# Broadcast rows of the decode states stored by batch row and given four buffers, and the decode rows of x turned in the first stage

## The chip, the cores and the metric

One of the eight cores of a Trainium2 chip runs the whole program. The metric is device time in microseconds (us), of the one core. Lower is better. The kernel before has a median of 3007.94 us over three runs (3006.08 to 3008.26).

## The reference, cut to what matters

The reference is one inference step of a hybrid decoder layer in float32: gated DeltaNet and S5 branches side by side, merged by gates, then an FFN. It runs for a prompt of 512 tokens and for a decode group of 8 rows with one token each. The part that the change touches is the DeltaNet state of the decode group:

```python
def step(S, inp):                       # gated_delta_recurrent, one token
    q_t, k_t, v_t, b_t, g_t = inp
    S = S * jnp.exp(g_t)[..., None, None]
    v_new = (v_t - jnp.einsum('bhk,bhkv->bhv', k_t, S)) * b_t[..., None]
    S = S + jnp.einsum('bhk,bhv->bhkv', k_t, v_new)
    return S, jnp.einsum('bhk,bhkv->bhv', q_t, S)
```

and the residual `x = x + merged @ w_out`, for which the 8 decode rows of x are needed with features on the partitions.

## The kernel before, in words

All activations lie with features on the 128 partitions and 520 columns: 512 prompt tokens and the 8 decode rows. A product with a weight matrix (`product`, L80 to L96) computes 128 output features at a time. `weights` (L72 to L79) loads a tile `raw` of 128x8x128 numbers (512 KB), ScalarE splits off its high part `whi` (L78) and VectorE its low part `wlo` (L70), and TensorE runs three matmuls for each of 8 row blocks and each half of the columns: 48 matmuls of 128x260 for 8 row blocks. There are three `raw` buffers, two of `whi` and `wlo`, and two PSUM tiles `pt`, so that a product can start only when the result of the one two places earlier has been taken out of PSUM.

The program runs in stages: the input is normed and turned into `hhi`/`hlo` (L151 to L203); products with `w_in` run beside the S5 and DeltaNet branches; then products with `w_glu`, with `w_br_s5` (eight tiles in `s5_part`, result `m`, L1176), with `w_br_dn` (result `gd`, L1274), with `w_out`, and the FFN by a Strassen scheme (L1363).

The decode states are the generator `decode` (L729 to L807), whose steps are laid between the `w_glu` and `w_br_s5` products. The new values `vn` [128 (v), 64 (h b)] are turned on TensorE (`pvt`), copied to `vr` and written to DRAM as `vsc` [h, b, v]. Then for each of 8 batch rows b:

- SyncE issues `vb <- vsc[:, b]` (L802): 8 runs of 128 floats (512 bytes), 4 KB apart in DRAM, read once for every partition, 512 KB in all. `vb` has 2 buffers.
- GpSimd multiplies `vb` by the keys (L803), VectorE adds it to the state tile `st` (L805), SyncE stores `st` (L806, 512 KB).

`st` of all eight rows is loaded and scaled (L804) before. A like copy stands earlier in `prep` (L946): `dx <- xdsc` spreads 16 rows of 4 KB in DRAM over eight groups of 16 partitions, the eight copies being the outermost loop of its source, 512 KB too; its rows serve as a price below. Each `gs` (L1174) is a gate tile of 260 KB. All DMAs are issued by SyncE, in one queue. After the decode, L1251 to L1259 load the 8 decode rows of x again (`xd`), turn them by 16 small transposes on TensorE (`pdx`) and copy them to `xdt`; L1293 adds them to the residual.

The order of each engine's instructions is fixed when the program is built: a scheduler lays out the recorded instructions, and each engine then runs its list in order. A wait at the head of such a list therefore holds all that stands behind it.

Of the kernel before, what the change touches and what calls it, by code (L numbers as in the profile page):

```python
# [9 lines left out]
F32 = mybir.dt.float32  # L10
# [7 lines left out]
P = 128  # L18
D = 2048
NTOK = 512  # L20
NB = 8
T = NTOK + NB
HF = T // 2
KD = D // P
# [9 lines left out]
def hybrid_step_kernel(  # L34
# [9 lines left out]
    nc = tc.nc  # L44
    V, G, A, PE = nc.vector, nc.gpsimd, nc.scalar, nc.tensor
    xp = x_prompt[0]
    xs = x_sample.rearrange("b l d -> (b l) d")
# [6 lines left out]
    dp = ctx.enter_context(tc.tile_pool(name="dp", bufs=1, space=DRAM))  # L54
# [5 lines left out]
    def slot(name):  # L60
        return big.tile([P, 8, T], F32R, tag="slot", name=name)

    def pmt(name="m", tag="m"):
        return pm.tile([P, 512], F32, tag=tag, name=name)
# [34 lines left out]
    ident = cp.tile([P, P], F32, name="ident")  # L99
# [42 lines left out]
            V.tensor_copy(vecs[:, 1, 0:25], pv[:, P:P + 25])  # L142


    HT = []
    hhi = [slot("hhi0"), slot("hhi1")]
    hlo = [slot("hlo0"), slot("hlo1")]
    for k in range(KD):
        HT.append((hhi[k // 8][:, k % 8], hlo[k // 8][:, k % 8]))
    with tc.tile_pool(name="x0", bufs=1) as x0:  # L150
        xt = [x0.tile([P, D], F32, name=f"x{c}") for c in range(5)]  # L151
        ss = x0.tile([P, 5, 2], F32, name="ss")
        junk = x0.tile([P, D // 2], F32, name="junk")
        G.memset(ss, 1.0)
        A.activation(junk[0:1, 0:1], ss[0:1, 0, 0:1], AF.Square)
        for c in (4, 0, 1, 2, 3):
            n = P if c < 4 else NB
            src = xp[c * P:(c + 1) * P, :] if c < 4 else xs
            for cs in (slice(0, D // 2), slice(D // 2, D)) if c < 4 else (slice(0, D),):
                nc.sync.dma_start(xt[c][0:n, cs], src[:, cs])  # L160
            if c == 0:
                load_vectors()
        for c in (4, 0, 1, 2, 3):
            n = P if c < 4 else NB
            for j in range(2):
                A.activation(junk[0:n], xt[c][0:n, j * D // 2:(j + 1) * D // 2], AF.Square,
                             accum_out=ss[0:n, c, j:j + 1])
            rs = ss[:, c, 0:1]
            V.tensor_tensor(rs, rs, ss[:, c, 1:2], ALU.add)
            V.tensor_scalar(rs, rs, 1.0 / D, EPS, op0=ALU.mult, op1=ALU.add)  # L170
            rsqrt(rs)
            if c == 4:
                V.tensor_scalar(xt[4][0:NB], xt[4][0:NB], rs[0:NB], None, op0=ALU.mult)
                continue
            for j in range(4):
                cs = slice(j * D // 4, (j + 1) * D // 4)
                V.tensor_scalar(xt[c][:, cs], xt[c][:, cs], rs, None, op0=ALU.mult)

        def turn(c):
            for k0 in range(0, KD, 2):  # L180
                pk = pmt("pk", "me"[k0 // 2 % 2])
                for j in range(2):
                    for i in range(2):
                        PE.transpose(pk[:, (j * 2 + i) * P:(j * 2 + i + 1) * P],
                                     xt[c + i][:, (k0 + j) * P:(k0 + j + 1) * P], ident)
                for j in range(2):
                    k = k0 + j
                    hi, lo = (v[:, c * P:(c + 2) * P] for v in HT[k])
                    pj = pk[:, j * 2 * P:(j + 1) * 2 * P]
                    A.activation(hi, pj, AF.Copy, scale=n1[:, k:k + 1])  # L190
                    V.scalar_tensor_tensor(lo, pj, n1[:, k:k + 1], hi.bitcast(F32), op0=ALU.mult, op1=ALU.subtract)

        pdec = pmt("pdec")
        for k in range(KD):
            PE.transpose(pdec[:, k * NB:(k + 1) * NB], xt[4][0:NB, k * P:(k + 1) * P], ident[0:NB, 0:NB])
        hd = x0.tile([P, KD, NB], F32, name="hd")
        V.tensor_tensor(hd, pdec[:, 0:KD * NB].rearrange("p (k b) -> p k b", b=NB),
                        n1.unsqueeze(2).to_broadcast([P, KD, NB]), ALU.mult)
        for i in range(2):
            A.activation(hhi[i][:, :, NTOK:T], hd[:, i * 8:(i + 1) * 8], AF.Copy)  # L200
            lo_part(hlo[i][:, :, NTOK:T], hd[:, i * 8:(i + 1) * 8], hhi[i][:, :, NTOK:T])
        turn(0)
        turn(2)  # L203
# [16 lines left out]
    def beta_decay():  # L220
        with tc.tile_pool(name="bap", bufs=1) as bp:
# [3 lines left out]
            A.activation(bc[:, 0], bc[:, 0], AF.Exp)  # L225
            pt = product(w_in, 0, C_BA, HT)
            bsb = bp.tile([16, T], F32, name="bsb")
# [254 lines left out]
    def u_tile(i, upp):  # L482
        pt = product(w_in, 0, C_U + i * P, HT, by_half=i == 0)
        us = gp.tile([P, T], F32, tag="gtile", name="us")
# [11 lines left out]
    def gate_tile(t):  # L496
        j, i = t // KD, t % KD
        pt = product(w_in, 0, (C_GD, C_GS)[j] + i * P, HT)
        gt = gp.tile([P, T], F32, tag="gate", name="gate")
# [229 lines left out]
    def decode(dec, dd, de, ohi, olo):  # L729
# [37 lines left out]
        vn = t64("vn")  # L767
# [20 lines left out]
        A.activation(ohi[:, :, NTOK:T], odv, AF.Copy)  # L788
        lo_part(olo[:, :, NTOK:T], odv, ohi[:, :, NTOK:T])

        pvt = pmt("pvt")
        PE.transpose(pvt[0:64, 0:P], vn, ident)
        vr = dd.tile([64, P], F32, name="vr")
        V.tensor_copy(vr, pvt[0:64, 0:P])
        vsc = dp.tile([8, 8, P], F32, name="vsc")
        nc.sync.dma_start(vsc.rearrange("h b v -> (h b) v"), vr)
        knv = kn.rearrange("p (h b) -> p h b", h=8)
        egv = decv[:, 0]
        for b in range(NB):
            st = sts[b]  # L800
            vb = de.tile([P, 8, P], F32, name="vb")
            nc.sync.dma_start(vb, vsc[:, b].unsqueeze(0).to_broadcast([P, 8, P]))  # L802
            G.tensor_tensor(vb, vb, knv[:, :, b:b + 1].to_broadcast([P, 8, P]), ALU.mult)  # L803
            V.tensor_tensor(st, st, egv[:, :, b:b + 1].to_broadcast([P, 8, P]), ALU.mult)  # L804
            V.tensor_tensor(st, st, vb, ALU.add)  # L805
            nc.sync.dma_start(s_dn_ssm[0, b].rearrange("h k v -> k h v"), st)  # L806
            yield  # L807
# [384 lines left out]
    fin = fin_s.enter_context(tc.tile_pool(name="fin", bufs=1))  # L1192
# [56 lines left out]
            A.activation(hi, src, AF.Copy, scale=scale)  # L1249
            V.scalar_tensor_tensor(lo, src, scale, hi.bitcast(F32), op0=ALU.mult, op1=ALU.subtract)  # L1250

    with tc.tile_pool(name="xdp", bufs=1) as xdp:
        xdt = fin.tile([P, KD, NB], F32, name="xdt")
        xd = xdp.tile([NB, D], F32, name="xd")
        nc.sync.dma_start(xd, xs)
        pdx = pmt("pdx")
        for k in range(KD):
            PE.transpose(pdx[:, k * NB:(k + 1) * NB], xd[:, k * P:(k + 1) * P], ident[0:NB, 0:NB])
        V.tensor_copy(xdt.rearrange("p k b -> p (k b)"), pdx[:, 0:KD * NB])  # L1259
    with tc.tile_pool(name="mp", bufs=8) as mp, tc.tile_pool(name="mq", bufs=2) as mq:  # L1260
        add_squares, rstd = squares(mq)
        for m in range(2):
# [21 lines left out]
            for t in range(KD):  # L1284
                a = acc(t)
                if m == 0:
                    xt = mq.tile([P, 4, P], F32, name="xt")
# [20 lines left out]
                else:  # L1308

                    q = t - 8  # L1310
                    b = acc(q)
# [116 lines left out]
    for q in range(8):  # L1428
        b = acc(q)
# [132 lines left out]
    with ExitStack():  # L1562
# [152 lines left out]
        for c in range(4):  # L1715
            for h in range(2):
                v = yt[c][:, h * D // 2:(h + 1) * D // 2]
# [41 lines left out]
```

## Time and profile before

| what | value |
|---|---|
| median of three runs | 3007.94 us |
| profiled execution, its own time | 3003.06 us |
| its span (first to last instruction) | 3001.3 us |
| TensorE busy | 2884.6 us, 96% |
| VectorE, ScalarE, GpSimd busy | 68%, 43%, 38% |
| mean granted TensorE clock | 0.979 |

The page of the profile gives busy shares and the chain that ended last: work followed back from the last instruction, at each step to what released it. The trace can be asked for one stretch, one engine or one tile. In its rows a time is microseconds from the start of the span; in brackets stands how long the engine was idle before, and what ended that. "DMA share" is the mean busy share of the 16 DMA engines. The profiled execution took 3003.06 us, 4.9 us (0.16%) less than the median.

### The profile page before, as it was taken

How to read it: one execution, taken by the hardware profiler on the slowest of the kernel's cores; microseconds unless marked ns; L12 is line 12 of the kernel's file. 1: busy time of each engine (PE TensorE's matmuls, PEld its weight loads, DVE VectorE, ACT ScalarE, POOL GpSimd, SP SyncE). 2: the span in 40 equal slices, each digit the busy share in tenths (PEclk: the TensorE clock that was granted, in tenths of full speed). 3: DMA queues.
4: the chain of work that ended last, by engine and by line, in shares of the span. 5: the costliest groups of instructions: out<-in, count | busy, mean ns of one | idle time of the engine just before them, and what ended most of it. 6: DMA issues, size and time to landing. Idle time of an engine off the chain costs nothing.

```text
span 3001.3 us, 60983 instructions
## 1 busy us (share of the span) xinstructions
PE 2884.6 (96%) x23869; PEld 2848.7 (95%) x23869; DVE 2043.5 (68%) x3405; ACT 1279.8 (43%) x2229; POOL 1132.9 (38%) x1656
## 2 busy tenths in 40 slices
PE   7999999899999999699998999999999999999997
PEld 7999999899999999699998999999999998999997
DVE  5767444344554334243458899999999988999997
ACT  5244433233333222022244555555555555445555
POOL 0674403654444300210133454555555444222233
PEclk9999999999999998899999999999999999999999
DMA  6454444223333364754444455555555548765542
GB/s 163 107 126 127 120 129 102 73 70 75 81 77 82 96 181 115 181 150 117 135 128 127 138 163 166 166 167 161 161 168 162 160 151 284 260 206 168 185 139 86
DMA packets 647701, 424.17 MB, mean 141 GB/s; under 512 B 66525, under 2 KB 597694, under 8 KB 643774
## 3 DMA queue, kind: packets, MB, share of 16 engines
q1 hardware_dynamic: 647414, 420.28, 48.4%
q8 instruction: 188, 3.08, 0.4%
q14 instruction: 99, 0.81, 0.1%
HBM read 342.85 MB, written 75.12 MB: 139 GB/s over the span
## 4 chain that ended last, share of the span: by engine, by line
PE 76%; POOL 8%; DMA 6%; DVE 5%; issue 2%; ACT 1%; SPq 1%; POOLq 0%; ACTq 0%; DVEq 0%
PE pt L94 30%; PE px L1363 23%; PE py L1363 12%; PE pz L1363 6%; POOL tm L953 2%; DVE wlo L70 2%; POOL uu L955 2%; DMA vb<-vsc 2%; DMA dx<-xdsc 2%; PE pss L904 1%; POOL et L598 1%; DVE ac L1635 1%; POOL et L597 1%; PE psk L761 1%; DVE sm L1352 0%
## 5 line engine op out<-in xcount | busy, mean ns | idle before, releaser
L70 DVE TENSOR_TENSOR wlo<-raw,whi 128x512 fp32r<-128x512 f32 (+1 forms) x485 | 523.9, 1095 | 241.5 <-ACT whi L78 194.4
L78 ACT ACTIVATE whi<-raw 128x1024 fp32r<-128x1024 f32 x218 | 231.0, 1060 | 669.0 <-PE pt L94 597.3
L94 PE MATMUL pt<-hhi,wlo 128*128 128x260 f32 (+2 forms) x2336 | 492.6, 289 | 2.7 <-DVE wlo L70 2.5
L94 PE MATMUL pt<-hlo,whi 128*128 128x260 f32 (+2 forms) x2336 | 493.2, 289 | 0.0
L94 PE MATMUL pt<-hhi,whi 128*128 128x260 f32 (+1 forms) x2336 | 490.2, 289 | 1.4 <-ACT pre L866 1.3
L94 PEld LDWEIGHTS pt<-hhi,wlo 128*128 128x128 f32 x2336 | 369.3, 191 | 6.3 <-DVE wlo L70 4.1
L94 PEld LDWEIGHTS pt<-hhi,whi 128*128 128x128 f32 x2336 | 367.6, 191 | 4.1 <-ACT pre L866 1.8
L94 PEld LDWEIGHTS pt<-hlo,whi 128*128 128x128 f32 x2336 | 369.9, 191 | 1.4 <-issue 0.2
L70 DVE TENSOR_TENSOR wlo<-s,whi 128x512 fp32r<-128x512 f32 (+1 forms) x272 | 312.7, 1163 | 4.3 <-ACT whi L1358 1.2
L1342 POOL TENSOR_TENSOR s<-raw 128x1024 f32<-128x1024 f32 (+1 forms) x90 | 217.3, 2415 | 254.9 <-DVE wlo L70 121.1
L1363 PE MATMUL px<-xT,whi 128*128 128x260 f32 x1408 | 257.6, 283 | 1.1 <-ACT u L1510 1.1
L1358 ACT ACTIVATE whi<-s 128x512 fp32r<-128x512 f32 (+1 forms) x272 | 167.8, 620 | 183.6 <-PE px L1363 101.1
L1358 ACT ACTIVATE whi<-raw 128x512 fp32r<-128x512 f32 (+1 forms) x267 | 166.2, 630 | 125.7 <-PE px L1363 68.8
L1363 PEld LDWEIGHTS px<-xT,whi 128*128 128x128 f32 x1408 | 217.1, 188 | 1.3 <-ACT u L1510 1.3
L1363 PE MATMUL px<-xT,wlo 128*128 128x260 f32 x704 | 199.0, 283 | 0.0
L1363 PE MATMUL px<-wx,whi 128*128 128x260 f32 x832 | 155.2, 284 | 3.9 <-ACT whi L1358 2.0
L1342 POOL TENSOR_TENSOR s<-raws 128x512 f32<-128x512 f32 (+1 forms) x64 | 80.3, 1257 | 193.0 <-DVE wlo L70 192.1
L1363 PE MATMUL pz<-xB,whi 128*128 128x260 f32 x704 | 131.3, 284 | 2.3 <-ACT whi L1358 2.3
L1363 PEld LDWEIGHTS px<-wx,whi 128*128 128x128 f32 x832 | 127.4, 188 | 5.7 <-ACT whi L1358 2.6
L1363 PEld LDWEIGHTS px<-xT,wlo 128*128 128x128 f32 x704 | 132.5, 188 | 0.0
L1363 PE MATMUL py<-xT,whi 128*128 128x260 f32 x704 | 129.9, 284 | 0.7 <-ACT whi L1358 0.7
L1363 PE MATMUL px<-xB,whi 128*128 128x260 f32 x704 | 129.5, 283 | 0.2 <-ACT whi L1358 0.2
(585 smaller groups left out, 7616.8 us busy)
## 6 DMA issues: line engine op xcount, KB each, us to landing
raw<-in_w_in_dram SPq DMA_DIRECT2D x146, 512.0 KB
raw<-in_w_ffn_gate_dram SPq DMA_DIRECT2D x88, 512.0 KB
raw<-in_w_ffn_up_dram SPq DMA_DIRECT2D x88, 512.0 KB
xT<-hx SPq DMA_DIRECT2D x88, 260.0 KB
raws<-in_w_ffn_down_dram SPq DMA_DIRECT2D x44, 512.0 KB
xB<-hx SPq DMA_DIRECT2D x66, 260.0 KB
raw<-in_w_out_dram SPq DMA_DIRECT2D x32, 512.0 KB
hs<-xT SPq DMA_DIRECT2D x12, 1040.0 KB
```

The source lines that it names most:

```text
L70: V.tensor_tensor(out, full, hi.bitcast(F32), ALU.subtract)
L78: A.activation(hi[:, :nk], raw[:, :nk], AF.Copy)
L94: PE.matmul(pt[:, h, 0:c1 - c0], w_[:, j], x[:, c0:c1], start=k == 0 and i == 0, stop=k == n - 1 and i == 2)
L597: G.tensor_tensor(t1[:, r, :, 0:n], E[:, r, :, 0:n], rr, ALU.mult)
L598: G.tensor_tensor(t2[:, r, :, 0:n], E[:, 1 - r, :, 0:n], ri, ALU.mult)
L761: PE.matmul(psk[:, 2 * i:2 * i + 2], sts[b][:, h], kqn[:, :, i], start=True, stop=True)
L904: PE.matmul(pss[:, s * 4 + c:s * 4 + c + 1], sq[:, s, c * P:(c + 1) * P], ones[:, 0:1], start=True, stop=True)
L953: G.tensor_tensor(tm[:, :, 0:31 - j], uu[:, :, j:j + 1].to_broadcast(sh), dx[:, j, j + 1:32].unsqueeze(1).to_broadcast(sh), ALU.mult)
L955: G.tensor_tensor(uu[:, :, j + 1:32], uu[:, :, j + 1:32], tm[:, :, 0:31 - j], ALU.add)
L1342: G.tensor_tensor(t, a, b, op)
L1358: A.activation(hi, w_in_, AF.Copy)
L1363: PE.matmul(o, w_[:, q - q0], x_, start=start and q == 0 and i == 0, stop=q == kp - 1 and i == 2, skip_group_check=not start)
```

## The change

- `vn` is first copied to `vp` with the order (b h) in place of (h b); `vsc` becomes [b, h, v], so that row b is one run of 1024 floats (4 KB), and the copy to 128 partitions reads this run once for each partition.
- `vb` has 4 buffers in place of 2.
- The 16 transposes of the decode rows of x stand in the first stage, where the rows are on the chip anyway. The result `xd0` is kept in DRAM as `xdtsc` (64 KB) and loaded to `xdt` after the decode.

```diff
+    xdtsc = dp.tile([P, KD, NB], F32, name="xdtsc")
...
             if c == 4:
+                pdx = pmt("pdx", "e")
+                for k in range(KD):
+                    PE.transpose(pdx[:, k * NB:(k + 1) * NB], xt[4][0:NB, k * P:(k + 1) * P], ident[0:NB, 0:NB])
+                xd0 = x0.tile([P, KD, NB], F32, name="xd0")
+                V.tensor_copy(xd0.rearrange("p k b -> p (k b)"), pdx[:, 0:KD * NB])
+                nc.sync.dma_start(xdtsc, xd0)
                 V.tensor_scalar(xt[4][0:NB], xt[4][0:NB], rs[0:NB], None, op0=ALU.mult)
...
+        vp = t64("vp")
+        V.tensor_copy(vp.rearrange("p (b h) -> p h b", b=NB), vn.rearrange("p (h b) -> p h b", b=NB))
         pvt = pmt("pvt")
-        PE.transpose(pvt[0:64, 0:P], vn, ident)
+        PE.transpose(pvt[0:64, 0:P], vp, ident)
...
-        vsc = dp.tile([8, 8, P], F32, name="vsc")
-        nc.sync.dma_start(vsc.rearrange("h b v -> (h b) v"), vr)
+        vsc = dp.tile([NB, 8, P], F32, name="vsc")
+        nc.sync.dma_start(vsc.rearrange("b h v -> (b h) v"), vr)
...
-            vb = de.tile([P, 8, P], F32, name="vb")
-            nc.sync.dma_start(vb, vsc[:, b].unsqueeze(0).to_broadcast([P, 8, P]))
+            vb = de.tile([P, 8, P], F32, name="vb", bufs=4)
+            nc.sync.dma_start(vb.rearrange("p h v -> p (h v)"),
+                              vsc[b].rearrange("h v -> (h v)").unsqueeze(0).to_broadcast([P, 8 * P]))
...
-        xd = xdp.tile([NB, D], F32, name="xd")
-        nc.sync.dma_start(xd, xs)
-        pdx = pmt("pdx")
-        for k in range(KD):
-            PE.transpose(pdx[:, k * NB:(k + 1) * NB], xd[:, k * P:(k + 1) * P], ident[0:NB, 0:NB])
-        V.tensor_copy(xdt.rearrange("p k b -> p (k b)"), pdx[:, 0:KD * NB])
+    xdt = fin.tile([P, KD, NB], F32, name="xdt")
+    nc.sync.dma_start(xdt, xdtsc)
```

The scheduler moves a few instructions on PE, DVE, ACT and SP within the first 60 us of the program and, around the decode, those below; GpSimd's list is the same. Line numbers are those of each kernel (L802, L805, L806, L1174, L1176 before are L811, L815, L816, L1184, L1186 after).

SyncE's list where the broadcasts begin (`raw` are weights, `out_dram<-st` the stores of the states), before:

```order
L76 DMA raw<-in_w_br_s_dram 128x8x128
L802 DMA vb<-vsc 128x8x128 x2
L1174 DMA gs<-gate_2_385 128x520
L1174 DMA gs<-gate_3_386 128x520
L1174 DMA gs<-gate_4_387 128x520
L76 DMA raw<-in_w_br_s_dram 128x8x128
L806 DMA out_dram<-st 128x8x128
L802 DMA vb<-vsc 128x8x128
L806 DMA out_dram<-st 128x8x128
L802 DMA vb<-vsc 128x8x128
```

and in the change:

```order
L76 DMA raw<-in_w_br_s_dram 128x8x128
L811 DMA vb<-vsc 128x1024 x3
L1184 DMA gs<-gate_2_406 128x520
L811 DMA vb<-vsc 128x1024
L1184 DMA gs<-gate_3_407 128x520
L1184 DMA gs<-gate_4_408 128x520
L76 DMA raw<-in_w_br_s_dram 128x8x128
L816 DMA out_dram<-st 128x8x128
L811 DMA vb<-vsc 128x1024
L816 DMA out_dram<-st 128x8x128
L811 DMA vb<-vsc 128x1024
```

Four broadcasts in place of two stand ahead of the next weight load, and each later one stands behind the store of a state four rows back.

VectorE's list at the same place (`st<-st,vb` adds a broadcast to a state, `m<-pt,gs` takes a product out of PSUM, `wlo` splits a weight tile), before:

```order
L805 TENSOR_TENSOR st<-st,vb 128x1024 x2
L1176 TENSOR_TENSOR m_14167<-pt,gs 128x520
L70 TENSOR_TENSOR wlo<-raw,whi 128x1024
L805 TENSOR_TENSOR st<-st,vb 128x1024
L1176 TENSOR_TENSOR m_14167<-pt,gs 128x520
L70 TENSOR_TENSOR wlo<-raw,whi 128x1024
```

and in the change:

```order
L815 TENSOR_TENSOR st<-st,vb 128x1024 x2
L1186 TENSOR_TENSOR m_14190<-pt,gs 128x520
L815 TENSOR_TENSOR st<-st,vb 128x1024
L70 TENSOR_TENSOR wlo<-raw,whi 128x1024
L815 TENSOR_TENSOR st<-st,vb 128x1024
L1186 TENSOR_TENSOR m_14190<-pt,gs 128x520
L70 TENSOR_TENSOR wlo<-raw,whi 128x1024
L815 TENSOR_TENSOR st<-st,vb 128x1024
L1186 TENSOR_TENSOR m_14190<-pt,gs 128x520
```

Before, one addition stood ahead of each product's result; now some have two, and the last of the eight stands ahead of the sixth result in place of the eighth.

SyncE's list where the decode ends (`gd` are gates of the next stage), before:

```order
L802 DMA vb<-vsc 128x8x128
L76 DMA raw<-in_w_br_dn_dram 128x8x128
L806 DMA out_dram<-st 128x8x128
L76 DMA raw<-in_w_br_dn_dram 128x8x128
L806 DMA out_dram<-st 128x8x128
L1255 DMA xd<-in_x_sample_dram 8x2048
L1267 DMA gd<-gate_0_367 128x520
```

and in the change:

```order
L816 DMA out_dram<-st 128x8x128
L76 DMA raw<-in_w_br_dn_dram 128x8x128
L816 DMA out_dram<-st 128x8x128
L76 DMA raw<-in_w_br_dn_dram 128x8x128
L1263 DMA xdt<-xdtsc 128x128
L76 DMA raw<-in_w_br_dn_dram 128x8x128
L1271 DMA gd<-gate_0_388 128x520
```

The load of the decode rows no longer stands directly behind the last store, and no TensorE instruction follows from it there.

## Rows read from the trace of the kernel before

**Rows 1.** The page, busy time, share of the span and instructions of each engine
```profile
PE 2884.6 (96%) x23869; PEld 2848.7 (95%) x23869; DVE 2043.5 (68%) x3405; ACT 1279.8 (43%) x2229; POOL 1132.9 (38%) x1656
```
**Rows 2.** Chain of waits, 1180 to 1285 us: shares, then start, us, what
```profile
by line: DMA vb<-vsc 55.4%; PE pt L94 15.5%; POOL vb L803 7.3%; issue 3.4%; DVE wlo L70 3.3%; DMA out_dram<-st 3.0%; DMA gd<-gate 2.9%; DVE st L805 2.4%; PE pdx L1258 1.8%; SPq L806 1.6%; DVE m L1176 1.3%; SPq L802 0.6%; SPq L1255 0.4%; SPq
...
1191.33 14.72 DMA vb<-vsc
...
1250.44 14.38 DMA vb<-vsc
```
**Rows 3.** Stretches: us, busy (x) of PE, PEld, DVE, ACT, POOL; PEclk, DMA share, GB/s
```profile
1188.06:1276.92 88.86, 64.79 (x448) 62.38 (x447) 27.84 (x35) 10.59 (x12) 16.27 (x9) 0.85 0.78 177
...
1340.00:1400.00 60.00, 60.00 (x506) 60.00 (x506) 18.02 (x19) 13.92 (x18) 0.00 (x0) 1.00 0.47 132
```
**Rows 4.** Chain of waits of the whole span: start, us, what
```profile
1345.20 5.75 PE pt L94 x48
```
**Rows 5.** Who waited for whom, 1188.06 to 1276.92: us, times, longest
```profile
POOL vb L803 <- DMA vb<-vsc: 58.6, 8, 9.2
...
DVE st L805 <- POOL vb L803: 49.5, 8, 8.1
PE pt L94 <- DVE m L1176: 13.7, 5, 3.5
```
**Rows 6.** Timeline of SyncE's issues: start, us, what [idle before <-releaser]
```profile
1190.27 0.38 SPq L76 DMA_DIRECT2D raw<-in_w_br_s_dram  x1
...
1271.55 0.30 SPq L1255 DMA_DIRECT2D xd<-in_x_sample_dram  x1
```
**Rows 7.** Timeline of GpSimd, second and eighth row of the batch
```profile
1206.12 1.91 POOL L803 TENSOR_TENSOR vb<-vb,kqn 128x1024 f32<-128x1024 f32 x1 [3.63 <-DMA vb<-vsc]
...
1264.96 1.92 POOL L803 TENSOR_TENSOR vb<-vb,kqn 128x1024 f32<-128x1024 f32 x1 [8.06 <-DMA vb<-vsc]
```
**Rows 8.** Stretches again, for DMA share and GB/s (the last two columns)
```profile
628.00:630.00 2.00, 2.00 (x23) 1.82 (x22) 1.51 (x2) 0.38 (x1) 0.00 (x0) 1.00 0.50 154
506.00:508.00 2.00, 2.00 (x19) 2.00 (x18) 1.93 (x5) 0.26 (x1) 0.00 (x0) 1.00 1.11 137
...
1258.00:1262.00 4.00, 2.76 (x13) 2.59 (x14) 1.89 (x3) 0.00 (x0) 0.00 (x0) 0.74 0.74 64
1264.00:1268.00 4.00, 2.06 (x18) 1.85 (x16) 1.09 (x1) 0.00 (x0) 1.92 (x1) 1.00 1.08 319
```
**Rows 9.** DMA queues: packets of 500 to 509 us, and of 1250 to 1265 us
```profile
DMA packets 1078, 0.99 MB, mean 110 GB/s; under 512 B 46, under 2 KB 950, under 8 KB 1078
...
DMA packets 4603, 2.34 MB, mean 156 GB/s; under 512 B 70, under 2 KB 4602, under 8 KB 4602
```
**Rows 10.** Chain of waits, 620 to 640 us
```profile
625.44 6.53 DMA dx<-xdsc
```
**Rows 11.** Timelines of DVE, PE and ACT in and behind the decode
```profile
1188.26 0.22 DVE L777 TENSOR_TENSOR qk<-vn,pq 128x64 f32<-128x64 f32 x1 [6.42 <-PE pq L776]
...
1195.01 0.43 PE L784 MATMUL pq<-ident,on 64*128 64x64 f32 x2
...
1256.64 1.06 ACT L78 ACTIVATE whi<-raw 128x1024 fp32r<-128x1024 f32 x1 [8.60 <-PE pt L94]
...
1275.07 1.84 PE L1258 MATMUL pdx<-ident,xd 8*128 8x8 f32 x16 [9.02 <-DMA gd<-gate]
...
1278.99 0.70 DVE L1274 TENSOR_TENSOR gd<-pt,gd 128x520 f32<-128x520 f32 x1 [1.74 <-PE pt L94]
```
**Rows 12.** Timelines of ACT and PE at the program's start
```profile
3.50 1.05 ACT L166 ACTIVATE junk<-x 8x1024 f32<-8x1024 f32 x1 [1.18 <-DMA x<-in_x_sample_dram]
...
7.32 0.45 PE L139 MATMUL pv<-ident,rows 128*128 128x128 f32 x1 [7.32 <-DMA rows<-in_norm_dram]
...
8.38 1.87 PE L195 MATMUL pdec<-ident,x 8*128 8x8 f32 x16 [0.38 <-DVE x L173]
...
21.38 1.07 ACT L78 ACTIVATE whi<-raw 128x1024 fp32r<-128x1024 f32 x1
```

More of the change, by code (lines that the diff above doesn't have):

```diff
@@ L1250, in put @@
             V.scalar_tensor_tensor(lo, src, scale, hi.bitcast(F32), op0=ALU.mult, op1=ALU.subtract)
-    with tc.tile_pool(name="xdp", bufs=1) as xdp:
-        xdt = fin.tile([P, KD, NB], F32, name="xdt")
-        xd = xdp.tile([NB, D], F32, name="xd")
-        nc.sync.dma_start(xd, xs)
-        pdx = pmt("pdx")
-        for k in range(KD):
-            PE.transpose(pdx[:, k * NB:(k + 1) * NB], xd[:, k * P:(k + 1) * P], ident[0:NB, 0:NB])
-        V.tensor_copy(xdt.rearrange("p k b -> p (k b)"), pdx[:, 0:KD * NB])
+    xdt = fin.tile([P, KD, NB], F32, name="xdt")
+    nc.sync.dma_start(xdt, xdtsc)
     with tc.tile_pool(name="mp", bufs=8) as mp, tc.tile_pool(name="mq", bufs=2) as mq:
```

## The prediction

> **What bounds the kernel now.** I read the page first: TensorE is busy 96% of the span [rows 1], so a change can win only where it is idle or slow. The chain of waits names such a place: from 1180 to 1285 us the broadcasts `vb<-vsc` hold 55% of the chain, four of the eight standing in it with some 14 us each [rows 2]. The table of stretches sizes it: from 1188.06 us, where the first `w_br_s5` product starts, to 1276.92 us, where the 16 transposes of the decode rows end, PE is busy 64.8 of 88.9 us at a mean clock of 0.85, while a later stretch of equal products is 60.0 of 60.0 us at 1.00 [rows 3]. The reader should see idle time of 24.1 us and, within the busy time, a lower clock after each gap.
>
> Why is PE idle there? The waits show a line of four: GpSimd waits 58.6 us for the broadcasts, VectorE 49.5 us for GpSimd, and PE 13.7 us for `m`, the copy out of PSUM, which stands behind the state addition in VectorE's list [rows 5]; last, PE is idle for 9.0 us before the transposes [rows 11]. So what ends last is a DMA. All DMAs are issued by SyncE into one queue, and the DMA engines are busy 0.78 of the stage [rows 3]: the queue is the bound here, and the question is what one broadcast costs in it.
>
> **The price of a broadcast before.** While the queue holds weights and stores it moves 319 GB/s, in a slow stretch like 1258 to 1262 us only 64 GB/s [rows 8]. So 512 KB of weights or stores cost 524,288 B / 319 GB/s = 1.64 us, a gate of 260 KB 0.83 us. GpSimd starts on the second row at 1206.12 us and on the eighth at 1264.96 us, each just released by its broadcast [rows 7]: 58.84 us. SyncE's list puts 6 broadcasts, 5 weight tiles, 6 stores and 6 gates into that time; the last three kinds take 11 x 1.64 + 6 x 0.83 = 23.0 us. That leaves 35.8 us, **6.0 us for each broadcast** of 512 KB. Counting back from 1206.1 us by two broadcasts and a weight tile, the queue began on the weights issued at 1190.27 us [rows 6] at 1206.1 - 12.0 - 1.6 = 1192.5 us.
>
> **The price after.** No row shows a copy of one 4 KB run to 128 partitions. The nearest is `dx`, which reads 16 rows of 4 KB eight times: 6.53 us from issue to landing [rows 10], 154 GB/s with half of the DMA engines busy while it is alone, and 137 GB/s with all busy when a weight load runs beside it [rows 8]. Its packets are whole: 1078 less 950 leaves 128 of 2 KB or more, one for each partition, where all of the broadcast's stretch but one are below 2 KB [rows 9]. At 154 GB/s a broadcast takes **3.4 us**, which I take, since it has the same run length and the same repeated reading. The bounds: 1.7 us, if all 16 engines work at the rate that `dx` gets from half of them (308 GB/s, near the 319 of weights), and 6.0 us, if only the repeated reading counts and not the run length. Above 6.0 us there is a rival, below.
>
> **The sum.** In the new list of SyncE, from that weight tile on to the first `w_br_dn` tile, stand 8 broadcasts, 5 weight tiles, 6 stores and 6 gates: 23.0 + 8p us. It lands at 1192.5 + 23.0 + 8 x 3.4 = 1242.7 us. ScalarE's `whi` takes 1.06 us [rows 11], the product 5.75 us at full clock [rows 4], and I add 1.7 us for the half clock after the gap: the clock of 0.85 over 88.86 us is 13 us lost, over eight gaps. The result `gd` is then taken at about 1251.4 us, against 1278.99 us before [rows 11]: **27.6 us less**. The lists behind it hold this: the eighth broadcast lands after 8p + 3 weight tiles, 4 stores and 4 gates, at 1234.5 us, its state addition ends some 3.3 us later and the sixth `m` behind it, which frees PSUM for the eighth product at 1238.5 us; that product ends at about 1246 us, before the first `w_br_dn` product needs to. Each later broadcast waits only for the state four rows back, with at least two broadcasts still in the queue, so four buffers leave no gap in it; alone, at the price of before, they would win nothing, as the queue is full already.
>
> What bounds the gain is PE: nine products of 5.75 us and two pairs of small matmuls of at most 0.43 us [rows 11] after 1188.1 us end at 1240.7 us. The ninth would start at 1234.9 us, so no price below (1234.9 - 1.1 - 1215.5) / 8 = 2.3 us helps further, and at most 38 us can go.
>
> The transposes at the end: 1.84 us of PE and the 9.0 us before them [rows 11] go with the stretch above and are not counted twice. The load was issued only at 1271.55 us, behind the last store's landing [rows 6]; the load of `xdtsc` waits for no such thing on PE, its reader is GpSimd's small copies eight products later. Next in line at that place are the gates `gd`, issued behind one more weight tile; I allow nothing for them, as the PSUM tiles cover one product.
>
> What is added: 16 transposes at the start, some 1.87 us like `pdec`; x of the decode rows is there at 3.50 us and PE idle until 7.32 us. The copy and SyncE's issue behind the sixth load of x put one DMA of 64 KB, 0.2 us, and a short issue ahead of the first weights; their first reader, at 21.38 us, follows on ScalarE's earlier work without a wait [rows 12]. For this and the moved rows of the first 60 us I take 0.5 us, between 0 and 1. The copy `vp`, some 0.22 us like its neighbour of 128x64, stands ahead of VectorE's idle time of 6.42 us before the step that follows [rows 11]: nothing, since that wait for PE covers it, and 0.22 us without it.
>
> Against the profiled execution's 3003.06 us the sum is 3003.1 - 27.6 + 0.5 = 2976.0 us. The median of the runs is 4.9 us higher, and I predict the median: **2981 us**. With p between 2.6 and 4.4 us it is 2974 to 2989 us.
>
> **Rivals.**
> 1. *PE is the bound.* If one copy keeps all 16 engines at the rate that half of them reach for `dx` (1.7 us), the queue is done at 1229 us and PE sets the end: 38 us less, 2970 us. For it: a DMA share of just 0.50 at 154 GB/s. Against: 137 GB/s with all of them busy [rows 8]. The Trainium skill gives a reason for the half (DMA: Bandwidth & Descriptors, section "Why a DMA increments its semaphore by 16 and not by 1"): a DMA is spread over the largest number up to 16 that divides the outermost size of both sides. By that rule `dx` with its 8 copies gets 8 engines, as the share of 0.50 agrees, and the new `vb` gets 16.
> 2. *The run length does not matter.* Weights also come in runs of 512 bytes and move at 319 GB/s, so short runs alone are not slow; it may be the one small region read 128 times, which stays. Then p = 6.0, the first `w_br_dn` tile lands at 1263.5 us, and only the end of the stage is better: 6.8 us less, 3002 us with the 0.5 us of the start. That the 4 KB are cut up again and the change doesn't do what it says would end here too; the 128 packets of `dx` speak against it. In the same page, section "Specifications", the skill puts line rate at transfers of 512 B and more: by that rule the longer run gains nothing, and the sum would be this one; the weights' rate agrees, but no run here shows the rule for a repeated source.
> 3. *Slower.* Before, an engine's reads go over 8 runs 4 KB apart; now all 16 engines read the same 4 KB at once. If that gets the rate of the slow stretch throughout, 64 GB/s, p = 8.2 us: the tile lands at 1281 us and the time is 3019 us. It decides from p = 6.8 us (no gain left), and from 7.6 us it is slower by over 0.2%. Against it: eight engines read the same rows for `dx` at 154 GB/s.
>
> **Chances.** The forecast 0.53, PE-bound 0.25, no gain from runs 0.16, slower 0.06. A measurement here can tell 0.2% (6 us) from no change; that is 3001.9 us. The second rival lies astride of it, with somewhat over half on the near side: faster 0.86, same 0.09, slower 0.05. The range goes from just under PE's bound to the near edge of the second rival: 2967 to 3000 us; what lies outside is most of the second and all of the third rival.
>
> **What would show it.** In the changed profile the stage from the first `w_br_s5` product to the first `gd` should take about 63 us in place of 91; packets of the broadcasts should be 4 KB, GpSimd's wait for them less than half of 58.6 us, and the wait of 9.0 us for the decode rows gone, PE's list running from one `w_br_dn` product to the next. Broadcasts that land every 4 us while alone prove the price; every 6 us, rival 2; PE without gaps and at full clock, rival 1. I am wrong if the stage shortens as said and the time does not, which would mean a loss in the first 60 us or behind the stage.

## The result, and the profile after

The changed kernel takes 2975.09 us, the median of four runs (2972.03 to 2978.72), against 3007.01 us for the kernel before beside it (3004.55 to 3008.26). The ratio is 0.9897, with a 95% interval of 0.9885 to 0.9909: 1.0% faster. The profiled execution took 2972.03 us, with a span of 2970.3 us, 31.0 us less than the span before. One execution of pitch_1024, a kernel of the experiments below, took 13,874.78 us, and is left out of that kernel's median.

The page of the changed kernel, the row that answers to [rows 1]: TensorE is busy for 5 us less than before, in a span that is 31 us shorter, so what went is mostly idle time.

```profile
PE 2879.3 (97%) x23869; PEld 2844.5 (96%) x23869; DVE 2055.2 (69%) x3406; ACT 1279.2 (43%) x2229; POOL 1137.2 (38%) x1656
```

The chain of waits of the changed kernel, 1180 to 1253 us, as shares. The broadcasts, 55% of the chain in [rows 2], are gone from it; what has come in their place is small, and it is VectorE: `st`, `wlo` and `olo`.

```profile
by line: PE pt L94 77.5%; issue 6.9%; DVE st L815 4.3%; DVE wlo L70 2.8%; DVE olo L70 2.6%; PE psk L768 2.6%; ACT whi L78 1.5%; DVE m L1186 0.9%; PE pq L791 0.5%; PE pq L787 0.3%; PE pq L783 0.2%; PE pvt L801 0.1%; DVEq L1186 0.0%; DVEq L81
```

The waits of the changed kernel, 1186 to 1278 us (us, times, longest): GpSimd waits 12.7 us for broadcasts in place of 58.6 [rows 5], and no row names the decode rows of x in front of TensorE.

```profile
POOL vb L813 <- DMA vb<-vsc: 12.7, 5, 4.9
```

VectorE's timeline at both ends of the stage. `qk`, at 1188.26 us in [rows 11], now marks its start at 1189.38 us, and the first `gd` comes at 1246.90 in place of 1278.99 us. From the one to the other it was 90.73 us and is 57.52 us: 33.2 us less. Ahead of the stage 1.1 us are lost, and behind it 1.1 us more (2970.3 - 1246.9 against 3001.3 - 1279.0), which makes the 31.0.

```profile
1189.38 0.22 DVE L784 TENSOR_TENSOR qk<-vn,pq 128x64 f32<-128x64 f32 x1 [5.50 <-PE pq L783]
...
1246.90 0.70 DVE L1278 TENSOR_TENSOR gd<-pt,gd 128x520 f32<-128x520 f32 x1 [3.69 <-PE pt L94]
```

The table of stretches, the changed kernel (columns as in [rows 3]). The stage's DMA share is 0.90, and TensorE is idle for 2.6 of 58.4 us where it was idle for 24.1 of 88.9 [rows 3].

```profile
1189.18:1247.60 58.42, 55.81 (x447) 55.06 (x447) 39.72 (x36) 11.55 (x13) 20.57 (x17) 0.97 0.90 275
```

The two losses of 1.1 us can't be laid to the change: in the kernels of the next section, whose edits all lie in the decode or in the first microseconds, the stage starts anywhere from 1187.7 to 1196.0 us, and the stretch behind it takes 1718 to 1725 us. The 0.5 us that I allowed for the start can't be seen either. By the timelines the first `w_in` product begins at 22.96 in place of 22.55 us, but a `whi` that started at 209.00 us before starts at 208.87 us now.

### The profile page after: what moved, and what is told of

The parts are those of the page before. It is cut to its first block, busy times and chain, and to the rows that moved or that the text cites. A ratio compares the mean times of both kernels' runs of the same rounds, so it can differ in the third digit from the quotient of the medians.

```text
span 2970.3 us, 60986 instructions
## 1 busy us (share of the span) xinstructions
PE 2879.3 (97%) x23869; PEld 2844.5 (96%) x23869; DVE 2055.2 (69%) x3406; ACT 1279.2 (43%) x2229; POOL 1137.2 (38%) x1656
## 4 chain that ended last, share of the span: by engine, by line
PE 77%; POOL 9%; DVE 6%; DMA 4%; issue 3%; ACT 1%; SPq 1%; POOLq 0%; ACTq 0%; DVEq 0%
PE pt L94 30%; PE px L1367 23%; PE py L1367 12%; PE pz L1367 6%; POOL tm L963 3%; POOL uu L965 2%; DVE wlo L70 2%; DMA dx<-xdsc 2%; PE psk L768 1%; PE pss L914 1%; DVE ac L1639 1%; POOL et L604 1%; POOL et L605 0%; DVE sm L1356 0%; PE pkq L944 0%
## 5 line engine op out<-in xcount | busy, mean ns | idle before, releaser
L94 PE MATMUL pt<-hhi,wlo 128*128 128x260 f32 (+1 forms) x2336 | 493.4, 289 | 4.1 <-DVE wlo L70 4.1
L94 PE MATMUL pt<-hlo,whi 128*128 128x260 f32 (+1 forms) x2336 | 493.6, 289 | 0.0
L70 DVE TENSOR_TENSOR wlo<-s,whi 128x512 fp32r<-128x512 f32 (+1 forms) x272 | 319.5, 1188 | 3.8 <-ACT whi L1362 0.7
L1367 PE MATMUL px<-xt,whi 128*128 128x260 f32 x704 | 129.3, 284 | 0.0
```

What stands on the lines that cost most here:

```text
L70: V.tensor_tensor(out, full, hi.bitcast(F32), ALU.subtract)
L94: PE.matmul(pt[:, h, 0:c1 - c0], w_[:, j], x[:, c0:c1], start=k == 0 and i == 0, stop=k == n - 1 and i == 2)
L1367: PE.matmul(o, w_[:, q - q0], x_, start=start and q == 0 and i == 0, stop=q == kp - 1 and i == 2, skip_group_check=not start)
```

## The experiments

All are compared with the kernel before, run beside them. "Stage" is the time from that `qk` to the first `gd`, from each kernel's own timeline of VectorE; "rate" is GB/s in a stretch where broadcasts make up most of what the queue moves (for the sources that can keep up with the rest, its first microseconds). These stretches are 2 to 14 us long, so a rate is not the price of every broadcast of its kernel. In xd_alone, old_source, pitch_2048 and pitch_8192 the first `gd` waits for a DMA, so their stages are a rough measure.

| kernel | source of a broadcast | median us | ratio (95%) | stage us | rate |
|---|---|---|---|---|---|
| before | 8 pieces of 512 B, 4096 B apart | 3007.01 | 1 | 90.73 | 64 [rows 8] |
| the change | 4 KB in one run | 2975.09 | 0.9897 (0.9885 to 0.9909) | 57.52 | 410 |
| layout_alone | 4 KB in one run | 2976.31 | 0.9895 (0.9876 to 0.9914) | 60.24 | |
| buffers_alone | 4096 B apart | 2998.24 | 0.9966 (0.9953 to 0.998) | 81.95 | |
| xd_alone | 4096 B apart | 2997.83 | 0.9964 (0.9952 to 0.9976) | 87.34 | |
| old_source | 4096 B apart | 2993.87 | 0.9945 (0.9919 to 0.9971) | 76.84 | 79 |
| cut_runs | 512 B apart | 2974.60 | 0.9883 (0.9868 to 0.9897) | 56.02 | 296 |
| pitch_1024 | 1024 B apart | 2971.66 (3 runs) | 0.9862 (0.9822 to 0.9902) | 58.77 | 267 |
| pitch_2048 | 2048 B apart | 2979.80 | 0.9901 (0.9876 to 0.9925) | 66.18 | 130 |
| pitch_4608 | 4608 B apart | 2975.08 | 0.9878 (0.9851 to 0.9906) | 56.17 | 291 |
| pitch_8192 | 8192 B apart | 3047.36 | 1.0129 (1.0106 to 1.0151) | 130.19 | 40 |
| mul_on_dve | 4 KB in one run | 2973.08 | 0.9873 (0.9847 to 0.9899) | 57.01 | |
| mul_on_act | 4 KB in one run | 2969.02 | 0.9867 (0.9847 to 0.9887) | 54.07 | |
| fused_on_dve | 4 KB in one run | 2975.61 | 0.9893 (0.9874 to 0.9912) | 58.20 | |

All of them compute the whole of the reference.

### Each part alone

layout_alone puts `vp` and the new `vsc` into the kernel before and keeps two buffers and the old `xd` (this diff is against the changed kernel):

```diff
-            vb = de.tile([P, 8, P], F32, name="vb", bufs=4)
+            vb = de.tile([P, 8, P], F32, name="vb")
```

> Kernel before with the layout alone: rows kept by batch row and head, 4 KB runs, two buffers, the old way of the decode rows of x. Theory (the run length sets the price of a broadcast): packets of 4 KB, a broadcast below 2 us while alone in the queue in place of 6.0, and most of the change's 32 us: 2976 to 2984 us. Rival (the buffers or the decode rows carry a share): with two buffers the queue waits for the addition two rows back, or the 16 transposes keep their wait of 9 us, and the time is 2988 us or more.

It came out at 2976.31 us, which is the theory's. The layout alone gives what the whole change gives; the two other parts together shorten the stage by another 2.7 us, which the medians can't tell from nothing.

buffers_alone is the kernel before with `bufs=4`:

> Kernel before with four buffers in place of two, nothing else. Theory: the queue is full already and each broadcast still costs 6.0 us, so nothing is won: 3004 to 3010 us. Rival (waiting for a free buffer is part of the 6.0 us): 3000 us or less.

2998.24 us, the rival's side: 10 us less. This contradicts the prediction's sentence that four buffers alone would win nothing. The waits of GpSimd in this kernel, 1186 to 1278 us, where it was 58.6 us [rows 5]:

```profile
POOL vb L803 <- DMA vb<-vsc: 39.0, 8, 8.9
```

The stretch of the stage in buffers_alone moves 202 GB/s at a DMA share of 0.73; the same stretch before moves 181 at 0.79 (the second fence). While more of these broadcasts stand in the queue at once, more bytes go through per busy microsecond. Why that is so, no run here tells.

```profile
1194.95:1277.80 82.85, 65.53 (x463) 63.60 (x463) 29.11 (x37) 11.54 (x13) 17.46 (x17) 0.86 0.73 202
```

```profile
1188.06:1279.69 91.63, 67.56 (x460) 65.14 (x460) 28.83 (x38) 11.65 (x13) 17.34 (x17) 0.84 0.79 181
```

SyncE's own waits tell a part of it. In the list of before, each broadcast from the third on stands behind the store of the state two rows back, and that store waits for VectorE's addition. At these stores (L806) SyncE waited for VectorE for 17.5 us before, from 1188 to 1280 us, and for 6.5 us in buffers_alone; the rows of before (us, times, longest):

```profile
SPq L806 <- DVE st L805: 8.8, 4, 3.3
SPq L806 <- DVE wlo L70: 8.7, 4, 2.8
```

So with two buffers the next broadcast was often issued late. How much of the 10 us that makes is not shown.

xd_alone is the changed kernel with the old source, without `vp`, and with two buffers:

> Kernel before with the decode rows of x turned in the first stage and kept in DRAM, nothing else. Theory: the queue still sets the stage; only the load and the transposes behind the last store go, 0 to 7 us: 3000 to 3007 us. Rival (the wait of 9.0 us before the transposes is a bound of its own, and the change's gain is in part here): 2998 us or less.

2997.83 us, just on the rival's side, and the trace bears out its first half: here the wait was a bound of its own. By the first `gd` its stage is only 3.4 us shorter, but that row misleads: this `gd` waits 4.90 us for its own gate from the queue, while TensorE has gone on with the next product.

```profile
1276.21 0.70 DVE L1275 TENSOR_TENSOR gd<-pt,gd 128x520 f32<-128x520 f32 x1 [4.90 <-DMA gd<-gate]
```

The sixth `gd` comes in both kernels when TensorE's products run evenly again. It starts 120.26 us after `qk` before (first row) and 112.26 us after it in xd_alone (second row; its `qk` starts at 1188.87 us):

```profile
1308.52 0.70 DVE L1274 TENSOR_TENSOR gd<-pt,gd 128x520 f32<-128x520 f32 x1 [1.94 <-PE pt L94]
...
1301.13 0.70 DVE L1275 TENSOR_TENSOR gd<-pt,gd 128x520 f32<-128x520 f32 x1 [1.94 <-PE pt L94]
```

That is 8.0 us, more than the 7.2 us between the two spans (2994.1 against 3001.3). So with slow broadcasts the early transposes are worth some 8 us, most of the wait of 9.0 us and the 1.84 us behind it [rows 11]. The gains of the parts don't add up: 32, 10 and 11 us alone, 32 us together, since each takes from the same idle time of TensorE.

### Is it the run length?

cut_runs is the changed kernel with rows of `vb` that stand 132 floats apart, so that nothing longer than 512 bytes can be moved in one piece:

```diff
-            vb = de.tile([P, 8, P], F32, name="vb", bufs=4)
+            vb = de.tile([P, 8, P + 4], F32, name="vb", bufs=4)[:, :, 0:P]
```

> The changed kernel with one edit: the rows of vb stand 132 floats apart on the chip, so that the same 4 KB of DRAM are read in pieces of 512 bytes. Theory (the run length sets the price): each broadcast costs some 6 us again, the first gd comes 15 us later or more, 2995 to 3007 us. Rival (the old source, 8 places 4 KB apart, was slow, not the short runs): price and time stay those of the change, 2972 to 2979 us.

This was meant to confirm my reason, and it overturns it. The packets from 1196 to 1202 us in the changed kernel (whole runs, nearly none below 2 KB) and then in cut_runs (nearly all below 2 KB):

```profile
DMA packets 769, 2.32 MB, mean 387 GB/s; under 512 B 83, under 2 KB 83, under 8 KB 769
```

```profile
DMA packets 3069, 1.55 MB, mean 259 GB/s; under 512 B 52, under 2 KB 3064, under 8 KB 3069
```

The runs are cut as intended, and the time is 2974.60 us, that of the change. Short runs have a price (259 against 387 GB/s), but not one that reaches the end of the stage. What made the old broadcasts slow must be where their pieces stood.

### Is it the distance between the pieces?

old_source is the control: the changed kernel with the source of before.

> The changed kernel with the source of before: vsc by head and batch row, 8 pieces of 512 bytes that stand 4096 bytes apart; four buffers and the early decode rows stay. All theories: slow, as the two edits that are left gave 10 and 11 us alone: 2986 to 2999 us, with stretches below 100 GB/s while broadcasts are in the queue. It is the control for the two kernels that follow.

2993.87 us, slow as expected. pitch_4608 changes one thing in it: nine rows for each head in place of eight, the ninth a copy that nobody reads (the copy of `vn` and the transpose ahead of `vsc` are widened to 72 rows for it; not shown).

```diff
-        vsc = dp.tile([8, 8, P], F32, name="vsc")
+        vsc = dp.tile([8, 9, P], F32, name="vsc")
```

> As old_source, but each head's rows are padded to nine, so that the 8 pieces of 512 bytes stand 4608 bytes apart. Theory A (pieces at places far apart are slow, whatever the distance): as old_source, 2986 to 2999 us. Theory B (the distance of exactly 4096 bytes puts the pieces in each other's way in DRAM): as fast as contiguous pieces, 240 GB/s or more while broadcasts are alone in the queue, 2972 to 2979 us.

2975.08 us, theory B. 512 bytes more between pieces of 512 bytes turn a broadcast from slow to fast. pitch_1024, pitch_2048 and pitch_8192 keep the order by batch row and head and put a gap behind each row:

```diff
-        vsc = dp.tile([NB, 8, P], F32, name="vsc")
+        vsc = dp.tile([64, 2, P], F32, name="vsc")
```

(`vsc[:, 0]` is written and read; 4 and 16 in place of 2 make the distances 2048 and 8192.)

> The changed kernel with the rows kept by batch row and head, but each row of 512 bytes followed by a gap of 512 bytes, so that the 8 pieces stand 1024 bytes apart within 8 KB. Theory A (any gap between pieces costs): between, 2980 to 2995 us. Theory B (only the distance of 4096 bytes): 2972 to 2979 us and 240 GB/s or more while broadcasts are alone in the queue.

> As pitch_1024, with a gap of 1536 bytes behind each row, so that the 8 pieces of 512 bytes stand 2048 bytes apart within 16 KB. If half of 4096 bytes is bad too: broadcasts below 200 GB/s while alone in the queue and 2978 to 2995 us. If only 4096 bytes (or its multiples) are: 240 GB/s or more, 2972 to 2979 us.

> As pitch_1024, with a gap of 7680 bytes behind each row, so that the 8 pieces stand 8192 bytes apart. If multiples of 4096 bytes are slow like 4096: stretches below 100 GB/s and 2986 us or more, as old_source. If 4096 bytes alone are slow: 2972 to 2979 us.

The rates, all from the table of stretches (the last two columns are DMA share and GB/s; TensorE is second, and in all but the last busy throughout). The change:

```profile
1200.00:1202.00 2.00, 2.00 (x19) 2.00 (x19) 2.00 (x2) 0.30 (x1) 2.00 (x2) 1.00 1.03 410
```

cut_runs, 512 bytes apart:

```profile
1200.00:1202.00 2.00, 2.00 (x19) 2.00 (x18) 2.00 (x2) 0.05 (x1) 0.98 (x1) 1.00 1.17 296
```

pitch_1024:

```profile
1200.00:1204.00 4.00, 4.00 (x33) 3.80 (x32) 0.94 (x4) 0.38 (x1) 0.71 (x1) 1.00 0.96 267
```

pitch_2048:

```profile
1200.00:1206.00 6.00, 6.00 (x53) 6.00 (x52) 4.96 (x4) 2.10 (x3) 2.48 (x2) 1.00 0.71 130
```

old_source, 4096 bytes apart:

```profile
1202.00:1204.00 2.00, 2.00 (x17) 1.80 (x16) 1.04 (x3) 0.77 (x1) 0.00 (x0) 1.00 0.72 79
```

pitch_4608:

```profile
1198.00:1202.00 4.00, 4.00 (x33) 3.79 (x32) 1.52 (x4) 1.21 (x2) 0.83 (x1) 1.00 1.10 291
```

pitch_8192:

```profile
1198.00:1212.00 14.00, 11.24 (x93) 10.97 (x91) 3.02 (x6) 3.32 (x4) 1.91 (x1) 1.00 0.22 40
```

The reader should see a fall with one exception. Up to 1024 bytes apart the rate is some 270 to 300 GB/s; in the stretches shown it is 130, 79 and 40 at 2048, 4096 and 8192; and 4608, between the two slowest, is back at 291. So theory B of pitch_1024 holds for 512 and 1024 bytes, but "only 4096" is too narrow. With pieces of the same size in all six, neither the length of a run nor the span of the region sets the rate, but the distance, and not by its size: of the distances tried, 2048, 4096 and 8192 are slow.

The order of the three slow ones is also that of the stages, 66.2, 76.8 and 130.2 us; that each doubling takes half of the rate is not shown. In old_source the neighbours of the stretch shown move 207 and 140 GB/s, and GpSimd starts on the second and third broadcast 3.2 and 3.3 us after the one before, each just released by it, which is some 160 GB/s; only later, issued one by one between stores, weights and gates, are they 5 to 10 us apart.

```profile
1207.12 1.92 POOL L810 TENSOR_TENSOR vb<-vb,kqn 128x1024 f32<-128x1024 f32 x1 [6.81 <-DMA vb<-vsc]
1210.36 1.92 POOL L810 TENSOR_TENSOR vb<-vb,kqn 128x1024 f32<-128x1024 f32 x1 [1.32 <-DMA vb<-vsc]
1213.67 1.91 POOL L810 TENSOR_TENSOR vb<-vb,kqn 128x1024 f32<-128x1024 f32 x1 [1.39 <-DMA vb<-vsc]
```

The DMA shares differ too, 0.71, 0.72 and 0.22, so the three are not slow in one and the same way. In whole time pitch_2048 can't be told from the change, as the intervals overlap; its stage is 8.7 us longer by the first `gd` and 6.3 us by the sixth. At 8192 GpSimd starts on the first two rows 13.0 us apart, which is 512 KB at 40 GB/s, and the kernel is 1.3% slower than the one before:

```profile
1209.61 1.91 POOL L812 TENSOR_TENSOR vb<-vb,kqn 128x1024 f32<-128x1024 f32 x1 [13.92 <-DMA vb<-vsc]
1222.61 1.91 POOL L812 TENSOR_TENSOR vb<-vb,kqn 128x1024 f32<-128x1024 f32 x1 [11.09 <-DMA vb<-vsc]
```

Why these distances are slow no run here shows; only the rates and times are shown. The Trainium skill (DMA: Bandwidth & Descriptors, section "Latency and other measured facts") tells of a like loss for rows 2 to 8 MB apart, cured by 4 KB of padding; the runs here show one from 2 KB on, where many partitions read the same pieces, and cured by 512 bytes.

### What is left above TensorE's work

In the changed kernel's stage TensorE has one gap, before the third product's first `wlo` matmul:

```profile
1210.99 0.51 PE L94 MATMUL pt<-ghi,wlo 128*128 128x260 f32 x2 [2.58 <-DVE wlo L70]
```

VectorE's timeline ahead of it shows why `wlo` is late, though its `whi` was ready at 1202.8 us: `olo`, 0.22 us before, takes 1.94 us, and two additions take 5.78 us together in place of 2.45.

```profile
1198.13 1.23 DVE L70 TENSOR_TENSOR wlo<-raw,whi 128x1024 fp32r<-128x1024 f32 x1 [0.15 <-ACT whi L78]
1199.27 1.94 DVE L70 TENSOR_TENSOR olo<-od,ohi 128x64 fp32r<-128x64 f32 x1
1201.16 5.78 DVE L815 TENSOR_TENSOR st<-st,vb 128x1024 f32<-128x1024 f32 x2
1206.87 0.69 DVE L1186 TENSOR_TENSOR m<-pt,gs 128x520 f32<-128x520 f32 x1
1207.48 2.32 DVE L815 TENSOR_TENSOR st<-st,vb 128x1024 f32<-128x1024 f32 x1
1209.72 1.21 DVE L70 TENSOR_TENSOR wlo<-raw,whi 128x1024 fp32r<-128x1024 f32 x1
```

GpSimd's timeline has four multiplications without a pause beside them:

```profile
1198.97 9.74 POOL L813 TENSOR_TENSOR vb<-vb,kqn 128x1024 f32<-128x1024 f32 x4 [4.86 <-DMA vb<-vsc]
```

The groups of instructions of the stage give the means (busy us, mean ns; then idle time and its cause), before, then after. Before, GpSimd multiplied while VectorE waited for it, so the two never met; now that the broadcasts come early, they run at once and both are slower.

```profile
L803 POOL TENSOR_TENSOR vb<-vb,kqn 128x1024 f32<-128x1024 f32 x8 | 15.3, 1916 | 58.6 <-DMA vb<-vsc 58.6
...
L805 DVE TENSOR_TENSOR st<-st,vb 128x1024 f32<-128x1024 f32 x8 | 9.8, 1225 | 49.5 <-POOL vb L803 49.5
```

```profile
L813 POOL TENSOR_TENSOR vb<-vb,kqn 128x1024 f32<-128x1024 f32 x8 | 18.6, 2335 | 12.7 <-DMA vb<-vsc 12.7
L815 DVE TENSOR_TENSOR st<-st,vb 128x1024 f32<-128x1024 f32 x8 | 17.0, 2134 | 0.0
```

Three kernels take the multiplication off GpSimd. mul_on_dve and mul_on_act:

```diff
-            G.tensor_tensor(vb, vb, knv[:, :, b:b + 1].to_broadcast([P, 8, P]), ALU.mult)
+            V.tensor_tensor(vb, vb, knv[:, :, b:b + 1].to_broadcast([P, 8, P]), ALU.mult)
```

```diff
-            G.tensor_tensor(vb, vb, knv[:, :, b:b + 1].to_broadcast([P, 8, P]), ALU.mult)
+            for h in range(8):
+                A.activation(vb[:, h], vb[:, h], AF.Copy, scale=kn[:, h * 8 + b:h * 8 + b + 1])
```

> The changed kernel with the multiplication of vb by the keys on VectorE in place of GpSimd. Theory (what is left above TensorE's work in the stage, some 5 us, comes from GpSimd and VectorE slowing each other: additions of 2.9 us in place of 1.2): the additions take 1.23 us each again, TensorE's gap near 1206 to 1211 us goes, and the time falls by 2 to 5 us to 2970 to 2973 us. Rival (8 multiplications of 1.23 us put 9.8 us more into VectorE's list ahead of the results of the products): no gain or a loss, 2974 to 2982 us.

> The changed kernel with the multiplication of vb by the keys on ScalarE, eight pieces of 128x128 a row with the key as a scale, in place of GpSimd. Theory (the gap of 2.6 us and the half clock behind it come from VectorE's additions, slowed by GpSimd, ahead of wlo): additions of 1.23 us, no gap of TensorE near 1206 to 1211 us, 2969 to 2973 us. Rival: the pieces stand ahead of whi in ScalarE's list and wait there for the first broadcast, so the gap stays or grows, 2974 to 2980 us.

fused_on_dve drops the multiplication and writes the addition as

```diff
-            V.tensor_tensor(st, st, vb, ALU.add)
+            for h in range(8):
+                V.scalar_tensor_tensor(st[:, h], vb[:, h], kn[:, h * 8 + b:h * 8 + b + 1], st[:, h], op0=ALU.mult, op1=ALU.add)
```

> The changed kernel with multiplication and addition in one instruction of VectorE for each head (eight of 128x128 a row) and none on GpSimd. Theory: eight such instructions take less than the 2.4 us of a separate multiplication and addition, so that the gap is smaller than the 2.3 us of mul_on_dve: 2970 to 2974 us. Rival: the fixed cost of small instructions eats that, 2974 to 2980 us.

mul_on_act gives 2969.02 us, the fastest of all; its profiled stage is 3.5 us shorter than that of the change. The same groups in it, and then its stretch of the stage: additions and `olo` are back at their old times, and TensorE is idle for 0.7 us at full clock throughout.

```profile
L816 DVE TENSOR_TENSOR st<-st,vb 128x1024 f32<-128x1024 f32 x8 | 9.8, 1225 | 10.3 <-ACT vb L814 10.3
...
L70 DVE TENSOR_TENSOR olo<-od,ohi 128x64 fp32r<-128x64 f32 x1 | 0.2, 215 | 0.0
```

```profile
1187.68:1242.65 54.97, 54.28 (x447) 53.56 (x447) 28.96 (x36) 30.18 (x77) 2.00 (x9) 1.00 0.93 292
```

Against the change's row that is 1.5 us less busy time (447 matmuls in both, the clock 1.00 in place of 0.97) and 1.9 us less idle time. Its median is 6.1 us below that of the change, but the intervals of the two ratios still touch (0.9887 and 0.9885), and 6 us is more than the stage gives. Of the stage's 3.5 us, the 1.9 us of idle time go with the multiplication. The 1.5 us of clock are not shown to: in cut_runs GpSimd multiplies as in the change and TensorE has the same gap, and yet its stage ran at full clock, with 54.31 us busy.

```profile
1212.80 0.51 PE L94 MATMUL pt<-ghi,wlo 128*128 128x260 f32 x2 [2.58 <-DVE wlo L70]
...
1190.99:1247.91 56.92, 54.31 (x447) 53.56 (x447) 36.16 (x36) 11.55 (x13) 22.61 (x17) 1.00 0.97 277
```

In mul_on_dve the additions take 1.22 us again, as the theory says, yet a gap of 2.32 us stays: VectorE can begin the first multiplication only when its broadcast is there, at 1201.65 us, and that one, an addition and a second multiplication stand ahead of `wlo` in its list. Its 2973.08 us is 2.0 us below the change, within what the runs can't tell apart. fused_on_dve has a gap of 2.62 us and 2975.61 us, the rival's case. So taking work off GpSimd is not enough; it has to go to an engine with time to spare, and in this stage that is ScalarE, busy for 11.6 of 58.4 us.

## Why the prediction came out as it did

**The time and the mechanism are two verdicts.** The forecast of 2981 us is 5.9 us above the measured median, and the range of 2967 to 3000 us holds that. But the reason that I gave for the new price, the length of the runs, is wrong.

- *The bound.* The broadcasts as the cause of the stage's length held: layout_alone removes most of the cost, and old_source brings much of it back. The queue as the only bound didn't: with the old source two more buffers gave 10 us, and the early transposes 11 us.
- *The price after.* The step that failed is "3.4 us, which I take, since it has the same run length and the same repeated reading". At 410 GB/s a broadcast takes 524,288 B / 410 GB/s = 1.3 us, below my lower bound of 1.7. And run length isn't what sets it: at 512 bytes it is 1.8 us. I read the packets of `dx` and of the broadcasts as the difference and did not ask about the 4 KB between the pieces, though it stands in the kernel's description and the third rival names it. The rows of `dx` are themselves 4096 bytes apart; whether that is why it gets 154 GB/s was not tried.
- *The sum.* From `qk` at 1188.3 us its form says 1192.5 + 23.0 + 8p + 1.1 + 5.75 + 1.7 - 1188.3, or about 35.8 + 8p, for the stage while the queue is the bound. Where it is: pitch_2048, with p = 524,288 B / 130 GB/s = 4.0, should take 68 us and takes 66.2; pitch_8192, with 13.1, 141 us and takes 130.2. But old_source, with 79 GB/s and p = 6.6, should take 89 us and takes 76.8: the rate of one slow stretch is not what a broadcast costs when several stand in the queue. And in all three the first `gd` waited for a DMA, not for TensorE's product as the sum has it, so the two hits are in part luck. The 1.7 us for the clock divides by eight gaps, where the trace before has six of over 1 us (five waits for `m` [rows 5] and the 9.0 us); it would be 2.2 us. The other limit held as well: "no price below 2.3 us helps further" fits that cut_runs and pitch_4608, at 1.8 us, are as fast as the change at 1.3.
- *Why the forecast was near all the same.* With the true price the sum falls to TensorE's bound, rival 1 and 2970 us. Two things that I had at nothing gave part of it back: the gap of 2.6 us, and 1.5 us of lower clock behind it. They make 4.1 us, and the result lies 5.1 us above that rival's figure. The forecast erred to the other side: a price too high by 2.1 us is 17 us over eight broadcasts, of which TensorE's bound let 10 count (38 us at most against my 27.6), and the two losses took 4 of these. That errors of opposite sign brought the forecast to within 6 us is luck.
- *Rival 1* described what happened better than the forecast: TensorE sets the end. The Trainium skill's rule that I put beside it (DMA: Bandwidth & Descriptors, section "Why a DMA increments its semaphore by 16 and not by 1") fits the DMA share of 1.03 at 410 GB/s.
- *Rival 2* was half right, that short runs aren't slow, and drew the wrong end from it: the small region read 128 times isn't slow either, when its pieces don't stand 2048, 4096 or 8192 bytes apart. The Trainium skill (DMA: Bandwidth & Descriptors, section "Specifications") has line rate from 512 B on; cut_runs agrees in so far as its pieces of 512 B cost the kernel nothing, though 259 against 387 GB/s shows that longer runs are still better.
- *Rival 3*, slower, needed 64 GB/s throughout. The new layout didn't do that, but pitch_8192 shows that the case exists, at 40 GB/s.
- *Four buffers.* "Alone, at the price of before, they would win nothing, as the queue is full already" is wrong: 10 us. A DMA share of 0.78 doesn't say whether the queue had work, as pitch_8192 shows with broadcasts in it at a share of 0.22; SyncE's waits for VectorE at the stores, 17.5 us, were at hand and said that it was fed late.
- *The decode rows of x.* The wait of 9.0 us went. On top of the layout it is worth little, as the prediction's sum has it: layout_alone is as fast as the change. Alone, with slow broadcasts, it was worth some 8 us (xd_alone). The price at the start, between 0 and 1 us, is not visible.
- *GpSimd.* I gave its list as unchanged and its work as free. Its list is unchanged, but when it runs is not: this is the cost that the change added, and it appeared in VectorE's durations, not in any wait.

## What to carry to other kernels

When a transfer is far below the rate of its neighbours, look at the distance between the places that it reads at the same time before the length of each: here a kernel with pieces 4096 bytes apart took 18.8 us longer than one with pieces 4608 bytes apart, and one padded row was worth as much as the new layout. Test a reason by an experiment that undoes it alone; a forecast that lands in its range proves nothing about why. And when a wait goes, ask which two engines will now run at the same time that used to take turns.

## What the runs showed of the hardware

In the stretches shown, the queue moved copies of eight pieces of 512 bytes in DRAM to 128 partitions at 296, 267, 130, 79 and 40 GB/s with the pieces 512, 1024, 2048, 4096 and 8192 bytes apart, and at 291 with 4608; with one run of 4 KB it moved 410.

VectorE's additions of 128x1024 took 2.13 us in the mean in place of 1.23 while GpSimd multiplied, and GpSimd's multiplications 2.34 in place of 1.92. The Trainium skill (SBUF — State Buffer, section "SBUF: two separate sides") says that the two share a pair of ports which one of them holds for a whole instruction, also where VectorE has two inputs in SBUF. The trace agrees: `olo`, which has two such inputs and takes 0.22 us alone, took 1.94 us, about as long as one multiplication.
